# Hybrid decoder layer on one core: GpSimd's work cut into parts, the decay chain kept together, weights split one unit ahead, small inverse roots as one power on GpSimd

## The chip, the cores and the metric

The kernel runs on one core of a Trainium2 chip. A core has a matrix engine (TensorE, PE in the rows), VectorE (DVE), ScalarE (ACT), GpSimd (POOL) and SyncE (SP), which only issues transfers here. Each engine runs its own instructions strictly in order, and waits on semaphores for the others. The metric is the device time of one launch in microseconds, lower is better.

## The reference, cut to what matters

One layer for a sequence of 1024 tokens and a model width of 1024, all in float32:

```python
mod = silu(c) @ w_ada + b_ada                 # 48 columns of 128: six vectors of 1024
h = rms_norm(x) * (1 + scale1) + shift1
gq, gk, gv, gz, ga, gb, sq, sk, sv = split(h @ w_in)
gq, gk, gv = silu(causal_conv4(gq, gk, gv))   # width 4, per channel
g = -exp(a_log) * softplus(ga + dt_bias); beta = sigmoid(gb)   # per token and head
o_g = rms_norm(gated_delta_rule(l2(gq), l2(gk), gv, g, beta)) * silu(gz)   # 8 heads, chunks of 64
o_s = sliding_window(rms_norm(sq), rms_norm(sk), sv)           # 8 query, 2 key heads, window 128
x = x + gate1 * (concat(o_g, o_s) @ w_out)
h2 = rms_norm(x) * (1 + scale2) + shift2
out = x + gate2 * ((silu(h2 @ w_gate) * (h2 @ w_up)) @ w_down) # hidden width 2816
```

## The kernel before

A float32 operand is **split** into a high part (ScalarE rounds it) and a low part (the operand minus the high part, `split`, L189 to L196), and each product is three matrix passes over them (`mm3`, L213 to L215). Weights come by SP's queue as 128x1024 tiles (`wunit`); ScalarE writes their high part, GpSimd subtracts for the low part.

Tokens are in two halves of 512 columns. The order of TensorE's work is written by hand: `dense` is a chain of generators, one per projection unit, `fill(n)` runs n steps of it, and between the fills stand the visits to the other work. The order on the other engines comes from a scheduler that follows dependencies, priorities (`high_priority`) and explicit edges (`issue_after`). The stages in time are: start with norm 1 (0 to 48 us), projections with convolution and per-chunk statistics (48 to 350), recurrence and window attention (350 to 600), output projection and norm 2 (600 to 780), FFN (780 to the end).

The names that the change touches:
- `rsqrt` (L176): an inverse square root as 11 VectorE instructions on a bit trick and three Newton steps. It is called for norms (`n1_0`, `n1_1`, `n2_0`, `n2_1`, 4 columns), the window keys (`sk`, 16), window queries (`s0` to `s3`, 16), delta-rule outputs (`o0` to `o7`, 8) and the pairs of delta-rule heads (`g0` to `g3`, 32 columns).
- `mod_col` (L248 to L260): one of the columns of `mod`. On VectorE it is one instruction (L254), on GpSimd a 128x1024 product (L257) that ScalarE sums (L258); then a 128x1 bias add on VectorE (L260). `ada_some` loads and works such columns, 32 of them after the start.
- `conv` (L362 to L372): takes a projection out of PSUM. ScalarE makes the first tap, VectorE the other three (L366), and for the second half a border of 1 to 3 columns from `tails` (L372).
- `token_gen` (L630 on): the decay `g`, 24 VectorE instructions of 128x64 on `tsc`, whose result `gt` (L662) goes into the matmuls `psg` (L667).
- `pair_gen` and its helpers: `ee` (L741 on GpSimd, L743 on VectorE), `kd` (L757), `aq` (L784), and `kq` times its decay row, one 128x2048 product on GpSimd (L791). `scale_rows` (L722 to L728): ScalarE spreads an inverse root to 128x512 (`wide_k`, `wide_s`), TensorE transposes it (`psr_k`, `psr_s`), VectorE multiplies. `key_gen`: `ssk`, its inverse root `rnk`, and `kdp` on GpSimd (L864).
- `wquery_gen`: `stq` (L712, L916), its inverse root `rnq`, then `scale_rows`, then the split `ql` on GpSimd.
- `out_proj` (`w_o`, `ps_o`), and `first_half` with `modulated`, of the second norm.

Of the kernel before, what the change touches and what calls it, by code (L numbers as in the profile page):

```python
# [8 lines left out]
F32 = mybir.dt.float32  # L9
# [8 lines left out]
P = 128  # L18
# [10 lines left out]
ADA_ITER = 14  # L29
ADA_DVE = ()  # L30
# [17 lines left out]
EPS = 1e-6  # L48
NEG = -1.0e30
# [5 lines left out]
def tile_hybrid_layer(  # L55
# [134 lines left out]
    def split(hi, lo, src, eng):  # L190

        act.activation(out=r(hi), in_=src, func=AF.Copy)  # L192
        last = eng.tensor_tensor(out=r(lo), in0=src, in1=hi, op=ALU.subtract)  # L193
        if eng is pool:
            done["pool"] = last
        return last  # L196

    def wunit(src, name, kt=KT, eng=None, parts=None, raw=None, steps=1):
# [51 lines left out]
    def mod_col(u, eng=dve, bias=True):  # L250
# [5 lines left out]
        else:  # L256
            eng.tensor_tensor(out=w, in0=w, in1=cb, op=ALU.mult)  # L257
# [6 lines left out]
    def ada_some(n, tag, eng=dve):  # L264
        for u in range(ada_next[0], ada_next[0] + n):
# [5 lines left out]
            mod_col(u, eng)  # L271
# [56 lines left out]
    def modulate(hi, lo, out, x, row, a, sh, eng):  # L328
# [5 lines left out]
        else:  # L334
            done["pool"] = eng.tensor_tensor(out=out, in0=x, in1=row, op=ALU.mult)
# [177 lines left out]
    queue[dve] = rstd_done["n1_0"]  # L513
# [123 lines left out]
    def token_gen():  # L637
# [19 lines left out]
        for n in (15, 13, 11, 9, 7, 5, 3):  # L657
# [4 lines left out]
        dve.scalar_tensor_tensor(out=gt, in0=lp, scalar=-1.0, in1=bc(ealog.unsqueeze(2), (P, H, NB)),  # L662
                                 op0=ALU.mult, op1=ALU.mult)
# [69 lines left out]
    def pair_stats(p):  # L733
# [7 lines left out]
        pool.tensor_tensor(out=ee, in0=ee, in1=bc(gtok[:, 2 * p:2 * p + 2].unsqueeze(3), (P, 2, NB, HD)), op=ALU.subtract)  # L741
# [15 lines left out]
        pool.tensor_tensor(out=kd, in0=kd, in1=bc(fk.rearrange("p j b -> p b j").unsqueeze(3), (P, NB, 2, HD)), op=ALU.mult)  # L757
# [11 lines left out]
    def pair_products(p):  # L769
# [21 lines left out]
        pool.tensor_tensor(out=kb8, in0=kb8, in1=bc(eg8, (P, 16, 2, HD)), op=ALU.mult)  # L791
# [58 lines left out]
    def key_gen():  # L850
# [9 lines left out]
        for v in range(2):  # L860
            ks.append(p8.tile([P, 2, T], F32, tag="s8", name=f"ks{v}"))
            kdp = t4(f"kdp{v}", (P, NB, 2, HD), tag="c")
            for dup in range(2):
                pool.tensor_tensor(out=kdp[:, :, dup], in0=ktok[:, :, v * HD:(v + 1) * HD],  # L864
                                   in1=bc(rnk3[:, :, v:v + 1], (P, NB, HD)), op=ALU.mult)
# [45 lines left out]
    def wquery_gen(p):  # L911
# [12 lines left out]
        pool.tensor_tensor(out=r(ql), in0=q, in1=qh, op=ALU.subtract)  # L924
# [744 lines left out]
```

## Time and profile before

| what | value |
|---|---|
| time, median of 3 runs | 1305.56 us (1302.16 to 1305.72) |
| the profiled execution's own time | 1303.1 us |
| its span on the core | 1301.3 us |
| mean granted TensorE clock | 0.954 of full speed |
| busy: PE, DVE, ACT, POOL | 1193.2, 911.2, 534.7, 477.2 us |

Times in the rows are microseconds from the span's start, durations microseconds unless ns stands there. A row of the timeline is: start, duration, engine, line, operation, written tile<-read tiles, shape, how many (several of the same in a row are one row with their sum), and in brackets how long the engine stood idle before it and what ended that. A duration holds what the instruction waited inside itself.

### The profile page before, as it was taken

The page shows a single profiled execution, that of the slowest core. Times are in us where ns is not written, and L with a number is a line of the kernel's source. Part 1 is how long each engine was busy: PE and PEld are TensorE (multiplying, and loading weights), DVE is VectorE, ACT ScalarE, POOL GpSimd, SP SyncE. Part 2 cuts the span into 40 slices and gives each one's busy share as a digit, 9 for nine tenths or more (in the row PEclk, how much of TensorE's full clock was granted, in tenths as well). Part 3 has the DMA queues.
Part 4 walks back from the last instruction along what each step waited for, and adds up shares of the span by engine and source line. Part 5 has one row for each costly group of instructions (what it writes and reads, how often), then busy time and mean ns, then how long its engine had stood idle before and what let it go on. Part 6 is the DMA issues. An engine that isn't in the chain of part 4 may idle for free.

```text
span 1301.3 us, 18727 instructions
## 1 busy us (share of the span) xinstructions
PE 1193.2 (92%) x6710; PEld 979.4 (75%) x6710; DVE 911.2 (70%) x1701; ACT 534.7 (41%) x973; POOL 477.2 (37%) x343
## 2 busy tenths in 40 slices
PE   6868697796899889999999889999999999999998
PEld 5757576685788677787777668888888888788887
DVE  7999889979724667577564668877788876566420
ACT  4373555422433867534453442222222233544430
POOL 4667354534425434345554430000000015465440
PEclk8898799898899899999999899999999999999999
DMA  8726458486638955433476886555445678876651
GB/s 328 230 94 261 159 119 220 137 218 219 180 116 195 168 90 128 154 125 130 159 235 226 289 277 206 194 192 199 167 162 191 202 253 304 292 273 200 206 166 41
DMA packets 173550, 250.62 MB, mean 193 GB/s; under 512 B 41361, under 2 KB 107153, under 8 KB 171921
## 3 DMA queue, kind: packets, MB, share of 16 engines
q1 hardware_dynamic: 163856, 241.03, 57.3%
q0 software_dynamic: 9600, 8.39, 4.0%
q8 instruction: 53, 0.87, 0.3%
q14 instruction: 41, 0.33, 0.1%
HBM read 182.89 MB, written 66.45 MB: 192 GB/s over the span
## 4 chain that ended last, share of the span: by engine, by line
PE 62%; DVE 6%; ACT 4%; DMA 3%; issue 2%; POOL 1%; SPq 0%; ACTq 0%; DVEq 0%; POOLq 0%
PE ps_S L1365 8%; PE ps_S L1364 8%; PE ps_S L1363 8%; PE ps_P L1364 5%; PE ps_P L1365 5%; PE ps_P L1363 5%; PE ps_c L1363 2%; PE ps_o L213 2%; PE ps_c L1364 2%; PE ps_c L1365 2%; PE ps_o L215 2%; PE ps_o L214 2%; PE ps_gz L213 1%; DVE soltmp L818 1%; PE ps_gz L215 1%
## 5 line engine op out<-in xcount | busy, mean ns | idle before, releaser
L193 POOL TENSOR_TENSOR wP<-rP,wP 128x512 fp32r<-128x512 f32 (+1 forms) x84 | 109.3, 1313 | 394.7 <-ACT wP L192 393.1
L1364 PE MATMUL ps_P<-t,wP 128*128 128x512 f32 x308 | 120.7, 392 | 0.9 <-DVE t L193 0.9
L1363 PE MATMUL ps_P<-t,wP 128*128 128x512 f32 x308 | 120.5, 391 | 0.1
L1365 PE MATMUL ps_P<-t,wP 128*128 128x512 f32 x308 | 120.2, 390 | 0.0
L192 ACT ACTIVATE wP<-rP 128x512 fp32r<-128x512 f32 (+1 forms) x84 | 47.6, 588 | 79.3 <-PE ps_P L1365 34.4
L1363 PE MATMUL ps_c<-B,w 128*128 128x512 f32 x176 | 70.3, 399 | 8.1 <-ACT X L1407 8.1
L1364 PE MATMUL ps_c<-B,w 128*128 128x512 f32 x176 | 69.5, 395 | 0.0
L1365 PE MATMUL ps_c<-B,w 128*128 128x512 f32 x176 | 69.4, 394 | 0.0
L1364 PEld LDWEIGHTS ps_P<-t,wP 128*128 128x128 f32 x308 | 57.8, 188 | 14.0 <-DVE t L193 1.8
L1363 PEld LDWEIGHTS ps_P<-t,wP 128*128 128x128 f32 x308 | 57.8, 188 | 13.1 <-ACT t L192 0.5
L1365 PEld LDWEIGHTS ps_P<-t,wP 128*128 128x128 f32 x308 | 57.8, 188 | 12.5
L1473 ACT ACTIVATE sg<-sg 128x512 f32<-128x512 f32 x33 | 20.9, 632 | 87.8 <-DVE sg L1469 87.8
L257 POOL TENSOR_TENSOR ada<-ada,cb 128x1024 f32<-128x1024 f32 x17 | 43.8, 2592 | 29.3 <-DMA ada<-in_ada_dram 18.7
L215 PE MATMUL ps_o<-mix,w_o 128*128 128x512 f32 x128 | 50.9, 398 | 2.6 <-POOL w_o L193 2.6
L213 PE MATMUL ps_o<-mix,w_o 128*128 128x512 f32 x128 | 52.4, 409 | 0.3 <-ACT w_o L192 0.3
L1550 DVE SCALAR_TENSOR_TENSOR x1r<-ps_P,modc,x1r 128x512 f32<-128x512 f32 x16 | 11.9, 747 | 56.3 <-PE ps_P L1365 56.3
L214 PE MATMUL ps_o<-mix,w_o 128*128 128x512 f32 x128 | 50.5, 394 | 0.0
L1363 PEld LDWEIGHTS ps_c<-B,w 128*128 128x128 f32 x176 | 33.7, 191 | 17.3 <-ACT X L1407 10.3
L1365 PEld LDWEIGHTS ps_c<-B,w 128*128 128x128 f32 x176 | 33.6, 191 | 7.2
L1364 PEld LDWEIGHTS ps_c<-B,w 128*128 128x128 f32 x176 | 33.6, 191 | 6.7
L1363 PE MATMUL ps_S<-T,wS2h 128*128 128x512 f32 x88 | 35.6, 405 | 2.1 <-ACT wS2h L192 2.1
L1469 DVE TENSOR_TENSOR ops<-ps_S,xu 128x512 f32<-128x512 f32 x22 | 15.2, 690 | 30.6 <-PE ps_S L1365 20.6
(521 smaller groups left out, 3686.5 us busy)
## 6 DMA issues: line engine op xcount, KB each, us to landing
ada<-in_ada_dram SPq DMA_DIRECT2D x48, 512.0 KB, 5.0
AD<-ops SPq DMA_DIRECT2D x11, 1536.0 KB, 6.1
w<-in_wgate_dram SPq DMA_DIRECT2D x44, 256.0 KB, 3.2
w<-in_wup_dram SPq DMA_DIRECT2D x44, 256.0 KB, 3.9
rP<-SD SPq DMA_DIRECT2D x16, 704.0 KB, 5.5
sd<-in_wdown_dram SPq DMA_DIRECT2D x20, 512.0 KB, 5.3
SD<-sd SPq DMA_DIRECT2D x20, 512.0 KB, 3.8
rP<-in_wdown_dram SPq DMA_DIRECT2D x12, 704.0 KB, 6.7
```

The costliest lines, as they stand in the source:

```text
L192: act.activation(out=r(hi), in_=src, func=AF.Copy)
L193: last = eng.tensor_tensor(out=r(lo), in0=src, in1=hi, op=ALU.subtract)
L213: pe.matmul(out, lhsT=r(lhs[0]), rhs=r(rhs[0]), start=first, stop=False)
L214: pe.matmul(out, lhsT=r(lhs[0]), rhs=r(rhs[1]), start=False, stop=False)
L215: pe.matmul(out, lhsT=r(lhs[1]), rhs=r(rhs[0]), start=False, stop=last)
L257: eng.tensor_tensor(out=w, in0=w, in1=cb, op=ALU.mult)
L818: dve.tensor_tensor(out=tv[g], in0=bc(L[:, i, i + 1:32].unsqueeze(1), (P, i, 31 - i)), in1=bc(L[:, 0:i, i:i + 1], (P, i, 31 - i)), op=ALU. ...
L1363: pe.matmul(ps, lhsT=r(wh), rhs=r(xh), start=first and i == 0, stop=False, **kw)
L1364: pe.matmul(ps, lhsT=r(wh), rhs=r(xl), start=False, stop=False, **kw)
L1365: pe.matmul(ps, lhsT=r(wl), rhs=r(xh), start=False, stop=i == n - 1, **kw)
L1469: done["U"] = dve.tensor_tensor(out=out, in0=ps, in1=other, op=ALU.add)
L1473: act.activation(out=out, in_=out, func=AF.Silu)
```

## The change

1. `rsqrt` of up to 16 columns is one GpSimd instruction, x to the power of a tile that holds -0.5. That concerns 17 calls (all but `g0` to `g3`).
2. GpSimd's larger products are issued in parts of 128x512: weight splits, `mod` columns, `ql`, `kd` in 2, `kq` in 4; `ee` per head. The FFN's splits, which are 128x512 or smaller already, stay.
3. The 32 bias adds of `mod` (L260) become one 128x32 add behind the last column.
4. The decay chain is issued with high priority after 11 fills, ahead of the rest of the `mod` columns; 8 pairs of columns stand before it.
5. Each weight unit's load and split are written one unit ahead of its use (`ahead`, and `nxt` in `out_proj`).
6. In the second norm all of `modulated` is on VectorE, behind a value of the output projection; 5 instead of 6 pieces of that projection go between.

```diff
+POW_MAX = 16
+    mhalf = cp.tile([P, 16], F32, name="mhalf")
+    pool.memset(mhalf, -0.5)
     def rsqrt(out, x, n, name):
+        if n <= POW_MAX:
+            return pool.tensor_tensor(out=out, in0=x, in1=mhalf[:, 0:n], op=ALU.pow)
...
+    def pool_tt(out, in0, in1, op, n):
+        m = out.shape[1] // n
+        for i in range(n):
+            s_ = slice(i * m, (i + 1) * m)
+            done["pool"] = pool.tensor_tensor(out=out[:, s_], in0=in0[:, s_], in1=in1[:, s_], op=op)
...
-            split(parts[0][:, ks_], parts[1][:, ks_], raw[:, ks_], eng or pool)
+            split(parts[0][:, ks_], parts[1][:, ks_], raw[:, ks_], eng or pool, 2)
...
-            eng.tensor_tensor(out=w, in0=w, in1=cb, op=ALU.mult)
+            pool_tt(w, w, cb, ALU.mult, 2)
...
-            mod_col(u, eng)
+            mod_col(u, eng, False)
...
+    def ahead(units):
+        get = lambda kind, p, halves=(0, 1), *_: wunit(wmain[BASE[kind] + p], f"w_{kind}{p}_{halves[0]}")
+        w = get(*units[0])
+        for i, u in enumerate(units):
+            nxt = get(*units[i + 1]) if i + 1 < len(units) else None
+            yield from proj(*u[0:2], u[2] if len(u) > 2 else (0, 1), w, *u[3:])
+            w = nxt
...
-        pool.tensor_tensor(out=ee, in0=ee, in1=bc(gtok[:, 2 * p:2 * p + 2].unsqueeze(3), (P, 2, NB, HD)), op=ALU.subtract)
+        for j in range(2):
+            pool_tt(ee[:, j], ee[:, j], bc(gtok[:, 2 * p + j].unsqueeze(2), (P, NB, HD)), ALU.subtract, 1)
...
-        pool.tensor_tensor(out=kb8, in0=kb8, in1=bc(eg8, (P, 16, 2, HD)), op=ALU.mult)
+        pool_tt(kb8, kb8, bc(eg8, (P, 16, 2, HD)), ALU.mult, 4)
...
-    for i in range(ADA_ITER):
+    for i in range(11):
         fill(VISITS_A[0])
-        with tc.issue_after(h_done[0].ins), tc.issue_after(h_done[1].ins):
-            ada_some(1, ADA_TAGS[2 * i], pool if i not in ADA_DVE else dve)
-            ada_some(1, ADA_TAGS[2 * i + 1])
-    next(token)
+        if i < ADA_FIRST:
+            with tc.issue_after(h_done[0].ins), tc.issue_after(h_done[1].ins):
+                ada_pair()
+    with tc.high_priority():
+        next(token)
+    with tc.issue_after(done["token"].ins):
+        for i in range(11, 14):
+            fill(VISITS_A[0])
+            for _ in range(3):
+                if ada_next[0] < 44:
+                    ada_pair()
...
+    dve.tensor_tensor(out=modc[:, 16:48], in0=modc[:, 16:48], in1=b_ada[:, 16:48], op=ALU.add)
...
     def out_proj(hf):
+        nxt = wunit(wout[0], f"w_o{hf}0")
         for dt in range(KT):
-            w = wunit(wout[dt], f"w_o{hf}{dt}")
+            w = nxt
+            if dt + 1 < KT:
+                nxt = wunit(wout[dt + 1], f"w_o{hf}{dt + 1}")
...
-            modulated(f1[k], k, 0, (dve, pool)[k % 2])
+            with tc.issue_after(done["x1"].ins):
+                modulated(f1[k], k, 0, dve)
...
-        for _ in range(6):
+        for _ in range(5):
```

TensorE's rows come out in the same order as before. On VectorE the decay chain (`tsc`) stood between other work; before, its middle read as follows (L658 are seven terms of the chain's series, L366 and L372 the convolution, L254 and L260 `mod` columns):

```order
L658 SCALAR_TENSOR_TENSOR tsc<-tsc 128x64
L254 ISA ada_1135,modc<-ada_1135,cb 128x1024
L254 ISA modc 128x1
L260 TENSOR_TENSOR modc<-modc,sml 128x1
L658 SCALAR_TENSOR_TENSOR tsc<-tsc 128x64
```

and of the change the end of the chain and what follows it (lines of the changed file: L677 is L658, L681 is L662, L378 and L384 the convolution, L266 the column):

```order
L674 TENSOR_TENSOR tsc<-tsc 128x64
L675 TENSOR_SCALAR tsc<-tsc 128x64
L677 SCALAR_TENSOR_TENSOR tsc<-tsc 128x64 x7
L678 SCALAR_TENSOR_TENSOR tsc<-tsc 128x64
L680 SCALAR_TENSOR_TENSOR tsc<-tsc 128x64
L681 SCALAR_TENSOR_TENSOR tsc<-tsc 128x64
L378 SCALAR_TENSOR_TENSOR kn_628<-ps_gk_1_1090,sml,kn_628 128x511
L384 SCALAR_TENSOR_TENSOR kn_628<-tails,sml,kn_628 128x1
```

The chain's 24 instructions now stand in one piece, and two convolutions with four columns that stood inside it come behind.

The second place is GpSimd at the first window query's inverse root (`rnq` from `stq`). Before, GpSimd had there

```order
L257 TENSOR_TENSOR ada_2592<-ada_2592,cb 128x1024
L257 TENSOR_TENSOR ada_2597<-ada_2597,cb 128x1024
L193 TENSOR_TENSOR w_sq_0_2824<-w_sq_0r,w_sq_0_2824 128x1024
L980 MEMSET tx_2934 32x8x32 x2
L257 TENSOR_TENSOR ada_2602<-ada_2602,cb 128x1024
```

and of the change (L182 is the power, L200 a part of a product)

```order
L200 TENSOR_TENSOR ada_2585<-ada_2585,cb 128x512 x2
L200 TENSOR_TENSOR ada_2590<-ada_2590,cb 128x512 x2
L182 TENSOR_TENSOR rnq_2675<-stq_2656,mhalf 128x16
L200 TENSOR_TENSOR w_sq_0_2696<-w_sq_0r,w_sq_0_2696 128x512 x2
L200 TENSOR_TENSOR ada_2595<-ada_2595,cb 128x512 x2
```

The power stands behind the two columns and ahead of the weights, and the 11 VectorE instructions of this root are gone from between the solve's instructions.

## Rows read from the trace of the kernel before

**Rows 1.** Page, part 1: busy time by engine.

```profile
PE 1193.2 (92%) x6710; PEld 979.4 (75%) x6710; DVE 911.2 (70%) x1701; ACT 534.7 (41%) x973; POOL 477.2 (37%) x343
```

**Rows 2.** Stage 48 to 350 us: busy us (count) by engine, TensorE's granted clock, DMA.

```profile
48.00:350.00 302.00, 241.87 (x1374) 202.76 (x1372) 271.64 (x543) 135.06 (x228) 152.40 (x74) 0.89 0.61 182
```

**Rows 3.** TensorE's waits, 60 to 360 us: total us, times, longest us.

```profile
PE psr_s L726 <- ACT wide_s L722: 13.6, 2, 13.4
PE psg L667 <- DVE tsc L662: 11.9, 1, 11.9
PE psr_k L726 <- ACT wide_k L722: 11.4, 2, 8.8
PE ps_gk L213 <- ACT kq L388: 8.6, 1, 8.6
PE ps_kd L871 <- DVE aq L784: 4.2, 1, 4.2
PE ps_skv L213 <- DVE qt L366: 2.4, 1, 2.4
```

**Rows 4.** TensorE's waits, 600 to 780 us.

```profile
PE ps_o L215 <- POOL w_o L193: 2.6, 2, 2.1
```

**Rows 5.** Instructions by line: count, shortest/median/longest ns, first and last start.

```profile
L372 DVE SCALAR_TENSOR_TENSOR kn<-tails,sml,kn x12: 204/210/2264, 106.7 to 220.7; 128x1 f32<-128x1 f32 x4, 128x2 f32<-128x2 f32 x4, 128x3 f32<-128x3 f32 x4
...
L260 DVE TENSOR_TENSOR modc<-modc,sml x32: 91/147/2352, 98.6 to 332.7; 128x1 f32<-128x1 f32 x32
...
L257 POOL TENSOR_TENSOR ada<-ada,cb x17: 2351/2405/3252, 85.1 to 320.3; 128x1024 f32<-128x1024 f32 x17
...
L193 POOL TENSOR_TENSOR wP<-rP,wP x84: 1012/1294/3168, 1062.9 to 1273.3; 128x512 fp32r<-128x512 f32 x56, 128x384 fp32r<-128x384 f32 x28
```

**Rows 6.** GpSimd's timeline, 97 to 350 us.

```profile
118.06 9.34 POOL L257 TENSOR_TENSOR ada<-ada,cb 128x1024 f32<-128x1024 f32 x4
...
214.50 4.60 POOL L791 TENSOR_TENSOR kq<-kq,egrow 128x2048 f32<-128x2048 f32 x1
...
251.03 4.57 POOL L791 TENSOR_TENSOR kq<-kq,egrow 128x2048 f32<-128x2048 f32 x1
...
311.80 5.21 POOL L257 TENSOR_TENSOR ada<-ada,cb 128x1024 f32<-128x1024 f32 x2 [10.20 <-DMA ada<-in_ada_dram]
```

**Rows 7.** VectorE's timeline, 118 to 330 us.

```profile
118.77 1.69 DVE L372 SCALAR_TENSOR_TENSOR kn<-tails,sml,kn 128x3 f32<-128x3 f32 x1
...
131.75 0.27 DVE L642 TENSOR_TENSOR tsc<-abt,rv 128x64 f32<-128x64 f32 x1 [0.24 <-ACT abt L353]
...
138.26 2.45 DVE L652 TENSOR_SCALAR tsc<-tsc 128x64 f32<-128x64 f32 x1
...
157.41 0.21 DVE L662 SCALAR_TENSOR_TENSOR tsc<-tsc 128x64 f32<-128x64 f32 x1
...
214.57 5.61 DVE L743 TENSOR_TENSOR ee<-ee,cmask 128x1024 f32<-128x1024 f32 x1 [2.13 <-POOL ee L741]
...
251.72 3.90 DVE L372 SCALAR_TENSOR_TENSOR v<-tails,sml,v 128x1 f32<-128x1 f32 x1
...
312.16 0.67 DVE L712 TENSOR_REDUCE stq<-sq_sq 128x8 f32<-128x512 f32 x1
...
328.66 0.16 DVE L186 SCALAR_TENSOR_TENSOR rnq<-rsq_s 128x16 f32<-128x16 f32 x1
```

**Rows 8.** TensorE's timeline around the decay matmuls `psg`.

```profile
145.37 0.39 PE L215 MATMUL ps_gk<-h,w_gk 128*128 128x512 f32 x1
157.67 0.69 PE L667 MATMUL psg<-tsc,tribd 128*128 128x64 f32 x2 [11.92 <-DVE tsc L662]
...
159.54 0.63 PE L215 MATMUL ps_gk<-h,w_gk 128*128 128x512 f32 x1
```

**Rows 9.** First inverse root at the start: its first and last VectorE instruction.

```profile
14.81 0.17 DVE L180 TENSOR_SCALAR rsq_n<-ms_n 128x4 int32<-128x4 int32 x1
...
16.59 0.16 DVE L186 SCALAR_TENSOR_TENSOR rs_n<-rsq_n 128x4 f32<-128x4 f32 x1
```

More of the change, by code (lines that the diff above doesn't have):

```diff
@@ L188, in rsqrt, with split @@
         return last
-    def split(hi, lo, src, eng):
+    def pool_tt(out, in0, in1, op, n):
[3 more added lines that the diff above has]
+            done["pool"] = pool.tensor_tensor(out=out[:, s_], in0=in0[:, s_], in1=in1[:, s_], op=op)
+    def split(hi, lo, src, eng, n=1):
         act.activation(out=r(hi), in_=src, func=AF.Copy)
-        last = eng.tensor_tensor(out=r(lo), in0=src, in1=hi, op=ALU.subtract)
         if eng is pool:
-            done["pool"] = last
-        return last
+            pool_tt(r(lo), src, hi, ALU.subtract, n)
+        else:
+            return eng.tensor_tensor(out=r(lo), in0=src, in1=hi, op=ALU.subtract)
     def wunit(src, name, kt=KT, eng=None, parts=None, raw=None, steps=1):
@@ L334, in modulate @@
         else:
-            done["pool"] = eng.tensor_tensor(out=out, in0=x, in1=row, op=ALU.mult)
+            pool_tt(out, x, row, ALU.mult, 1)
             act.activation(out=r(hi), in_=out, func=AF.Identity, scale=a, bias=sh)
@@ L512, in tile_hybrid_layer @@
         rs = rstd(ps, "n1_0")
-    queue[dve] = rstd_done["n1_0"]
+    queue[pool] = rstd_done["n1_0"]
     keep_warm(WARM[1])
@@ L661, in token_gen @@
         dve.scalar_tensor_tensor(out=lp, in0=lp, scalar=2.0, in1=xa, op0=ALU.mult, op1=ALU.add)
[L662 to L663 removed]
+        done["token"] = dve.scalar_tensor_tensor(out=gt, in0=lp, scalar=-1.0, in1=bc(ealog.unsqueeze(2), (P, H, NB)),
+                                                 op0=ALU.mult, op1=ALU.mult)
         yield
@@ L863, in key_gen @@
             for dup in range(2):
-                pool.tensor_tensor(out=kdp[:, :, dup], in0=ktok[:, :, v * HD:(v + 1) * HD],
-                                   in1=bc(rnk3[:, :, v:v + 1], (P, NB, HD)), op=ALU.mult)
+                pool_tt(kdp[:, :, dup], ktok[:, :, v * HD:(v + 1) * HD], bc(rnk3[:, :, v:v + 1], (P, NB, HD)), ALU.mult, 1)
             yield
@@ L880, in tile_hybrid_layer @@
     token, keys = token_gen(), key_gen()
-    dense = chain(first, *(proj(kind, 2, (hf,), w_2[i]) for hf in range(2) for i, kind in enumerate(("gk", "gq"))), *(skv_unit(i) for i in range(4, NB)), proj("gk", 0, (1,)), proj("gq", 0, (1,)),
-                  proj("gk", 1, (1,)), proj("gq", 1, (1,)), proj("gk", 3), proj("gq", 3),
-                  *(proj("gv", p) for p in range(4)), *(proj("sq", p) for p in range(4)), proj("gz", 0, tags=("u",)), proj("gz", 1, tags=("u",)),
+    dense = chain(first, *(proj(kind, 2, (hf,), w_2[i]) for hf in range(2) for i, kind in enumerate(("gk", "gq"))), *(skv_unit(i) for i in range(4, NB)),
+                  ahead([(kind, p, (1,)) for p in range(2) for kind in ("gk", "gq")] + [("gk", 3), ("gq", 3)]
+                        + [(kind, p) for kind in ("gv", "sq") for p in range(4)]
+                        + [("gz", p, (0, 1), ("u",)) for p in range(2)]),
                   two_units((("gz", 2), ("gz", 3)), ("u",)))
@@ L923, in wquery_gen @@
         act.activation(out=r(qh), in_=q, func=AF.Copy)
-        pool.tensor_tensor(out=r(ql), in0=q, in1=qh, op=ALU.subtract)
+        pool_tt(r(ql), q, qh, ALU.subtract, 2)
         pool.dma_start(out=QS[0, p], in_=r(qh))
@@ L950, in tile_hybrid_layer @@
         if visit is v3:
-            for i in range(32 - 2 * ADA_ITER):
+            for i in range(48 - ada_next[0]):
                 ada_some(1, "b", pool if i % 4 else dve)
+    dve.tensor_tensor(out=modc[:, 16:48], in0=modc[:, 16:48], in1=b_ada[:, 16:48], op=ALU.add)
     dve.scalar_tensor_tensor(out=a2, in0=modc[:, 32:40], scalar=1.0, in1=n2w, op0=ALU.add, op1=ALU.mult)
@@ L1211, in out_proj @@
             sp.dma_start(out=x, in_=xT[dt, :, half(hf)])
-            dve.scalar_tensor_tensor(out=x, in0=ps, scalar=modc[:, 16 + dt:17 + dt], in1=x, op0=ALU.mult, op1=ALU.add)
+            done["x1"] = dve.scalar_tensor_tensor(out=x, in0=ps, scalar=modc[:, 16 + dt:17 + dt], in1=x,
+                                                  op0=ALU.mult, op1=ALU.add)
             if dt == 0:
```

13 lines of the change are left out of this document (7 added, 6 removed).

## The prediction

> **What bounds the kernel now.** I read the page's busy times first. TensorE is busy for 92% of the span, the others for at most 70% [rows 1]. So the time can fall in two ways only: where TensorE stands idle, and where its clock is granted at half. The change removes no matmul. Next I read the windows by stage. In the stage from 48 to 350 us TensorE is busy for 241.87 of 302.00 us at a mean granted clock of 0.89, while VectorE is busy for 271.64 us, that is 90% [rows 2]. Here VectorE is the bound, and GpSimd works beside it for 152.40 us. Then I read TensorE's waits in this stage: the window queries' spread inverse root (13.4 us in one piece), the decay chain (11.9), the pairs' spread inverse root (8.8 and 2.6), a projection's bank behind a convolution (8.6, and 2.4 more at the query convolution, with a second wait of that length at the key convolution), and the AQ product (4.2) [rows 3]. Every one ends on VectorE, or on a ScalarE step that VectorE released. Last I read why VectorE is late: its instructions with two operands from the on-chip memory are long only while GpSimd runs. A border step of the convolution takes 204 ns at its shortest and 2264 ns at its longest, a 128x1 bias add 91 and 2352 ns [rows 5]; the long ones are as long as a GpSimd product, 2405 ns for 128x1024 [rows 5]. The timelines show it directly. While GpSimd runs four columns from 118.06 for 9.34 us [rows 6], VectorE's border step takes 1.69 us [rows 7]; against the 4.60 us product of `kq` at 214.50 [rows 6], `ee` at 214.57 takes 5.61 us; against the one at 251.03 [rows 6], a 128x1 step takes 3.90 us [rows 7]. So VectorE waits for the end of GpSimd's instruction, and about one VectorE instruction gets in per boundary between two of GpSimd's.
>
> By the Trainium skill, "SBUF — State Buffer", section "Who interferes with whom", a VectorE instruction with two SBUF inputs contends with a GpSimd instruction that reads SBUF, as a lock for the whole instruction. The trace agrees: 3.90 us instead of about 0.2.
>
> **The change part by part.** The sum is made against the profiled execution, 1303.1 us, which lies 2.5 below the median of the runs.
>
> *Parts of 512.* A 128x512 part takes about 1.29 us (the median of the FFN's splits, which are that size) where a 128x1024 product takes 2.41 [rows 5], so two parts cost 0.18 us more on GpSimd, which has room (152.40 of 302 us [rows 2]). What VectorE waits at most falls from 2.4 to 1.3 us, and at `kq` from 4.6 to 1.3. Bounds: nothing, if each VectorE instruction merely waits twice as often, and the whole wait at the other end. By place: the product of `kq` in four saves `ee` about 4.6 - 1.3 = 3.3 us, and with the 16-column root of `sk` gone from among VectorE's rows some 0.7 more (four or five steps of 0.16 [rows 9]), so 4 of the 8.8 us at `psr_k`. The other `psr_k` wait, 2.6 us, falls by 1.5. At 251.72 a 128x1 step falls from 3.90 to at most about 1.3 + 0.2, so 2.8 of the 4.2 us at `ps_kd` go. The two waits of 2.4 us at the convolutions fall by 3.5 together, since every border step there waits for one product (1.69 us) and would wait for a part, and the bias adds between are gone. The wait of 8.6 us falls by 1.5; it hangs on VectorE's second half of `h` too, which stays.
>
> *The decay chain.* It begins at 131.75 and ends at 157.41 + 0.21, 25.9 us for 24 instructions of some 0.21 us, or 5 us of work; three are held for 2.3 to 2.5 us, as at 138.26 (2.45), and the rest of the time goes to convolutions and columns that stand between [rows 7]. TensorE comes to `psg` at 157.67 - 11.92 = 145.75 [rows 8]. In one piece the chain needs about 5 us, some 3 for the ScalarE steps in it (an estimate), and waits behind GpSimd's parts: with 4 to 6 of these, 5 to 8 us. So it ends 13 to 16 us after 131.75, at 145 to 148. The wait falls from 11.9 to about 2: a gain of 10. Bounds: if all 24 waited for a part of 1.29 us it would end at 131.75 + 5 + 31 = 168, 10 us later than now; but that needs 24 parts of GpSimd's work ready in that time, and the columns are held back behind the chain. With no wait it gains the whole 11.9. What is late next: the two convolutions of `kn` and `qt` that stood inside the chain now come behind it, and their PSUM banks come free some 3 us later. Among TensorE's waits only those of 8.6 and 2.4 us are for such a bank [rows 3]; I put 2 us on it.
>
> *The inverse roots on GpSimd.* 17 calls take 187 VectorE instructions away and add 17 on GpSimd. At the start the 11 instructions run from 14.81 to 16.59 + 0.16, that is 1.94 us [rows 9]. No row shows a power on GpSimd. Bounds: 0.16 us, as one such VectorE instruction [rows 9], and 2.41, a whole 128x1024 product [rows 5]. I take 1 us, between, since it has at most 16 columns but is another operation. Where it matters is `s0`: the sums are ready at 312.16 + 0.67, the root only at 328.66 [rows 7], 15.8 us later, since the 11 steps alternate with the solve's and wait for GpSimd. As one instruction it stands on GpSimd behind two columns that run from 311.80 for 5.21 us [rows 6], in four parts then. So it starts at about 317.5 and ends at 318.5, where it now ends at 328.66 + 0.16: 10.3 us earlier, of the 13.4 us that TensorE waits behind it [rows 3]. Since what stands ahead on GpSimd also waits for a transfer of its own (10.20 us [rows 6]), I count 7. Calls `s1` to `s3` and `o0` to `o7` lie under other matmuls, and their VectorE work is hidden as before; nothing for them. At the start I put 0, with 1 either way.
>
> *Weights a unit ahead.* TensorE waits for weights for 2.6 us at `ps_o` [rows 4] and nowhere else that matters: 2. *The bias adds*: their price is in the waits above. *The second norm's edit*: four 128x512 products go from GpSimd to VectorE, which is idle for 30% of the span [rows 1]; nothing, and up to 4 x 0.67 = 2.7 us against it (by the 128x512 reduction at 312.16 [rows 7]) if TensorE waits there.
>
> *The sum.* Idle time: 1.5 + 3.5 + 10 + 1.5 + 4 + 2.8 + 7 + 2 = 32.3. Behind a wait the clock is at half for some microseconds: a matmul at 159.54 takes 0.63 us, at 145.37 0.39 [rows 8], 0.24 us apart. With three waits gone for good, at some five or six matmuls each, 4 is an estimate for it. Against that stand 2 for the convolutions behind the chain and 8 for what I can't place: power and parts in GpSimd's queue ahead of `ee`, `kd` and `kdp`, and the stage's work moving closer to VectorE's own limit (271.64 us of work and waits in a stage that would last 275 [rows 2], of which the waits must shrink for it to fit). 1303.1 - 32.3 - 4 + 10 = 1276.8. I say 1277.
>
> **The rivals.**
> *The waits are only dealt out anew* (0.17). VectorE then waits twice as often for half as long; only what leaves VectorE counts: the roots of `s0` (7), part of the chain's regrouping (5), weights (2). 1303 - 14 + 4 for the parts' cost = 1293. For it: one VectorE instruction gets in at each boundary [rows 6, 7]. Against: at `kq` a single instruction waits for 4.6 us, and a second wait doesn't follow.
> *The power is dear* (0.08). Slower: it ends on the other side if one power holds GpSimd, and with it VectorE, for long. Some eight calls stand on TensorE's path (norms, `sk`, `s0`, and the outputs that come last). To eat the 26 us, each must cost 2 + 26/8 = 5.3 us; at 7 us, three times the dearest row above, the time is 1277 + 8 x 5 = 1317 less what is hidden, about 1312. Nothing in the rows is that dear on GpSimd save `kq`'s 4.60.
> By the Trainium skill, "GPSIMD Engine Reference", section "2.1 Instruction dispatch", the first call of a freshly loaded GpSimd routine pays about 6 us for its code; no run here shows it. By that the start alone would be some 5 us longer, 1282.
> *Banks behind the chain* (0.10). The convolutions that come behind it, and the columns behind those, make TensorE wait for PSUM where it did not: the 10 us come back. 1287. For it: such waits of 8.6 and 2.4 us exist [rows 3].
> *The change does not do what it says* (0.07). The products in parts still hold VectorE and the power waits behind transfers in GpSimd's queue, as the 10.20 us do [rows 6]: 1301 to 1304.
>
> **How the numbers follow.** The forecast has 0.58, the rivals 0.17, 0.08, 0.10 and 0.07. A measurement of this kernel tells about 0.3% from no change, that is 3.9 us around 1305.6. The forecast and the cases at 1287 and 1293 are faster: 0.85, less 0.01 for their upper ends. Same: 0.09, most of the case without effect and some of the dear power. Slower: 0.07. The forecast's own range is 1264 to 1288: 8 more if all waits named go, 11 less if the upper bounds of power and parts hold. The range for all is 1260 to 1302, which leaves out the slow case and the best.
>
> **What would show it.** In the changed profile the wait at `psg` is at most 4 us; the longest wait of `psr_s` is at most 6; `ee` takes at most 3 us on VectorE; no 128x1 step takes over 1.5; the power rows on GpSimd are about 1 us; the granted clock from 48 to 350 us rises to about 0.93. It is wrong if a power takes over 3 us, if VectorE's border steps still take 2 us, or if a new wait on PSUM banks stands behind the chain.

## The result and the profile after

The changed kernel takes 1287.07 us (median of 4 runs, 1285.41 to 1288.89) against 1303.86 for the kernel before (4 runs): a ratio of 0.9876, with a 95% interval of 0.9853 to 0.9900. It is faster by 16.8 us in the medians, 13 to 19 us by the interval. The forecast was 1277 with a range of 1264 to 1288, so the direction is right, the time lies 1 us inside the upper end of the range, and 10 us of the expected gain are missing.

Page, part 1 of the changed kernel, which answers to [rows 1]:

```profile
PE 1192.2 (93%) x6710; PEld 980.0 (76%) x6710; DVE 855.9 (66%) x1487; ACT 534.5 (42%) x973; POOL 525.9 (41%) x434
```

VectorE has 55 us less, GpSimd 49 us more. The window of the stage from 48 to 350 us, which answers to [rows 2]:

```profile
48.00:350.00 302.00, 253.96 (x1486) 211.20 (x1485) 251.21 (x474) 141.30 (x238) 188.28 (x140) 0.92 0.65 191
```

TensorE does 12 us more in the same stretch, and its mean granted clock rises from 0.89 to 0.92. TensorE's waits of the changed kernel between 60 and 345 us (in us: total, times, longest), which answer to [rows 3]:

```profile
PE pst L697 <- ACT gst L691: 10.4, 1, 10.4
PE psr_k L745 <- ACT wide_k L741: 8.5, 2, 7.0
PE psr_s L745 <- ACT wide_s L741: 7.6, 2, 6.1
PE ps_gk L225 <- ACT kq L400: 7.6, 1, 7.6
PE ps_gk L227 <- POOL w_gk L200: 3.6, 1, 3.6
PE pst_sq L728 <- DVE qs L747: 2.8, 2, 2.0
PE ps_gk L225 <- ACT w_gk L204: 1.6, 1, 1.6
...
PE pst L697 <- ACT gst L690: 1.2, 1, 1.2
...
PE psg L686 <- DVE tsc L681: 0.8, 1, 0.8
PE ps_kd L890 <- DVE aq L804: 0.3, 1, 0.3
```

The decay chain's wait at `psg` fell from 11.9 to 0.8 us, `ps_kd` from 4.2 to 0.3, `psr_s` from 13.4 to 6.1, and the two convolution waits are gone. But at the top stands a wait that did not exist: 10.4 us at `pst`, the transposes of `gst`, which VectorE and ScalarE make from the result of `psg`. Also new are 3.6 + 1.6 us for the weights `w_gk`.

TensorE's rows are in the same order in both kernels, so the start of the same matmul can be compared. The table is from both timelines of TensorE:

| matmul | before, us | after, us | earlier by |
|---|---|---|---|
| `ps_skv` behind the query convolution | 125.97 | 117.50 | 8.5 |
| `ps_gk`, third pass, waits for `w_gk` | 141.97 | 137.49 | 4.5 |
| `psg` | 157.67 | 145.11 | 12.6 |
| second `pst` | 162.84 | 160.63 | 2.2 |
| `psr_k`, the long wait | 229.30 | 224.84 | 4.5 |
| `ps_kd` behind `aq` | 257.03 | 244.97 | 12.1 |
| first `psr_s` | 329.54 | 307.58 | 22.0 |
| second `psr_s` | 345.45 | 329.65 | 15.8 |
| `ps_S` behind `wS2h` | 778.25 | 764.43 | 13.8 |
| end of the span | 1301.3 | 1287.2 | 14.1 |

The gain comes in four steps (the convolutions before 126 us, the decay chain up to `psg`, the pairs from 185 to 260, the root `s0`), and three times a part of it is handed back: 4.0 us at `w_gk`, 10.4 of 12.6 us between `psg` and `pst`, and 6.2 us behind `s0`. Behind 345 us nothing more is gained: 15.8 us there, 14.1 at the end.

Why `pst` is late stands in VectorE's timeline of the changed kernel (L681 ends the chain, L378 and L384 are convolutions, L266 are columns, L688 is the copy from `psg` into `gst`):

```profile
144.83 0.23 DVE L681 SCALAR_TENSOR_TENSOR tsc<-tsc 128x64 f32<-128x64 f32 x1
144.98 0.74 DVE L378 SCALAR_TENSOR_TENSOR kn<-ps_gk,sml,kn 128x511 f32<-128x511 f32 x1
145.64 0.21 DVE L384 SCALAR_TENSOR_TENSOR kn<-tails,sml,kn 128x1 f32<-128x1 f32 x1
145.76 1.22 DVE L266 CUSTOM_DVE_ANT_0 ada<-ada,cb 128x1024 f32<-128x1024 f32 x1
...
154.64 1.22 DVE L266 CUSTOM_DVE_ANT_0 ada<-ada,cb 128x1024 f32<-128x1024 f32 x1
155.78 0.08 DVE L266 DVE_READ_ACCUMULATOR2_ANT modc<- 128x1 f32 x1
155.78 0.74 DVE L378 SCALAR_TENSOR_TENSOR qt<-ps_gq,sml,qt 128x509 f32<-128x509 f32 x1
156.44 0.21 DVE L384 SCALAR_TENSOR_TENSOR qt<-tails,sml,qt 128x3 f32<-128x3 f32 x1
156.57 0.21 DVE L688 COPY gst<-psg 128x64 f32<-128x64 f32 x1
```

`psg` runs at 145.11, but the copy of its result stands behind two convolutions and six columns and starts at 156.57: what was taken out of the chain now stands between the chain's result and its first use. Why TensorE waits for `w_gk` stands in GpSimd's timeline, where 14 column parts are ahead of its split. The split itself begins 2.1 us earlier than before (136.16 against 138.25), but TensorE comes to it 8.4 us earlier. Two later rows of the same view are read further below:

```profile
115.75 20.46 POOL L200 TENSOR_TENSOR ada<-ada,cb 128x512 f32<-128x512 f32 x14
136.16 2.50 POOL L200 TENSOR_TENSOR w_gk<-w_gk_1r,w_gk 128x512 fp32r<-128x512 f32 x2
...
303.79 3.07 POOL L182 TENSOR_TENSOR rnq<-stq,mhalf 128x16 f32<-128x16 f32 x1
306.83 7.36 POOL L200 TENSOR_TENSOR w_sq<-w_sq_0r,w_sq 128x512 fp32r<-128x512 f32 x2
```

The power, and VectorE's border step and `ee`, by line (count, shortest/median/longest ns, first and last start), the latter two answering to [rows 5, 7]:

```profile
L182 POOL TENSOR_TENSOR fo<-so,mhalf x8: 1635/1644/1683, 383.8 to 563.1; 128x8 f32<-128x8 f32 x8
L182 POOL TENSOR_TENSOR rs_n<-ms_n,mhalf x4: 1006/1014/1033, 16.0 to 633.0; 128x4 f32<-128x4 f32 x4
L182 POOL TENSOR_TENSOR rnq<-stq,mhalf x4: 2926/3002/3175, 303.8 to 357.8; 128x16 f32<-128x16 f32 x4
...
L384 DVE SCALAR_TENSOR_TENSOR kn<-tails,sml,kn x12: 205/620/1303, 106.1 to 215.9; 128x1 f32<-128x1 f32 x4, 128x2 f32<-128x2 f32 x4, 128x3 f32<-128x3 f32 x4
...
L763 DVE TENSOR_TENSOR ee<-ee,cmask x4: 1209/2172/2306, 178.5 to 229.5; 128x1024 f32<-128x1024 f32 x4
```

A power costs 1.0, 1.6 and 3.0 us for 4, 8 and 16 columns (the 17th call, the keys' `rnk`, 2.90). The border step's longest wait fell from 2.26 to 1.30 us, the length of a part, and its median rose from 0.21 to 0.62: it waits more often for less. `ee` takes at most 2.31 us where it took 5.61.

### The profile page after: what moved, and what is told of

The parts are those of the page before. It is cut to its first block, busy times and chain, and to the rows that moved or that the text cites. A ratio compares the mean times of both kernels' runs of the same rounds, so it can differ in the third digit from the quotient of the medians.

```text
span 1287.2 us, 18639 instructions
## 1 busy us (share of the span) xinstructions
PE 1192.2 (93%) x6710; PEld 980.0 (76%) x6710; DVE 855.9 (66%) x1487; ACT 534.5 (42%) x973; POOL 525.9 (41%) x434
## 4 chain that ended last, share of the span: by engine, by line
PE 61%; DVE 19%; DMA 10%; ACT 5%; issue 2%; SPq 2%; POOL 1%; DVEq 0%; ACTq 0%; POOLq 0%
PE ps_S L1404 7%; PE ps_S L1402 7%; PE ps_S L1403 7%; PE ps_P L1403 5%; PE ps_P L1402 5%; PE ps_P L1404 5%; PE ps_o L225 2%; PE ps_o L227 2%; PE ps_o L226 2%; PE ps_c L1402 2%; PE ps_c L1403 2%; PE ps_c L1404 2%; DVE ada L458 1%; DMA rP<-in_wdown_dram 1%; DMA sd<-in_wdown_dram 1%
## 5 line engine op out<-in xcount | busy, mean ns | idle before, releaser
L200 POOL TENSOR_TENSOR wP<-rP,wP 128x512 fp32r<-128x512 f32 (+1 forms) x84 | 110.1, 1324 | 394.7 <-ACT wP L204 393.3
L200 POOL TENSOR_TENSOR ada<-ada,cb 128x512 f32<-128x512 f32 x34 | 50.5, 1517 | 19.1 <-DMA w_gz_0r<-in_wmain_dram 10.7
L1589 DVE SCALAR_TENSOR_TENSOR x1r<-ps_P,modc,x1r 128x512 f32<-128x512 f32 x16 | 11.9, 747 | 54.6 <-PE ps_P L1404 54.6
L1404 PE MATMUL ps_S<-T,wS2l 128*128 128x512 f32 x88 | 35.6, 404 | 1.0 <-DVE wS2l L208 1.0
```

Source lines behind the costliest of these rows:

```text
L200: done["pool"] = pool.tensor_tensor(out=out[:, s_], in0=in0[:, s_], in1=in1[:, s_], op=op)
L1404: pe.matmul(ps, lhsT=r(wl), rhs=r(xh), start=False, stop=i == n - 1, **kw)
L1589: dve.scalar_tensor_tensor(out=x, in0=src, scalar=g2(dt), in1=x, op0=ALU.mult, op1=ALU.add)
```

## The experiments

My theory: the parts carry the gain, and the missing 10 us are the pieces handed back at `pst` and at `w_gk`, each because an instruction that TensorE needs stands behind columns in its engine's queue. The rival: the stage is bound by what VectorE and GpSimd have to do together, so any regrouping only moves the waits. Every time below stands with its ratio to the kernel before, measured on the same chip, and the 95% interval of the ratio; the changed kernel's ratio is 0.9876 (0.9853 to 0.9900). Starts of matmuls are read from one profiled execution of each kernel. Executions of one kernel lie up to 11 us apart (e15: 1287.49 to 1298.53), so the end of one trace counts for less than the ratio.

**e1: the late columns behind `gst`.**

```diff
-        dve.tensor_tensor(out=ed.rearrange("p h b -> p (h b)"), in0=psg[:, 64:128], in1=gst[:, 2], op=ALU.subtract)
+        done["gst"] = dve.tensor_tensor(out=ed.rearrange("p h b -> p (h b)"), in0=psg[:, 64:128], in1=gst[:, 2],
+                                        op=ALU.subtract)
...
             fill(VISITS_A[0])
-            for _ in range(3):
-                if ada_next[0] < 44:
-                    ada_pair()
...
             next(visit)
+        if n_visit == 0:
+            with tc.issue_after(done["gst"].ins):
+                while ada_next[0] < 44:
+                    ada_pair()
```

> The changed kernel, with the last six pairs of mod columns issued behind VectorE's ed (the instruction behind the copy of psg into gst) instead of behind the decay chain; everything else as changed. Theory: the 10 us that the chain gave at psg came back at pst (10.4 us), because the copy into gst stands on VectorE behind six columns of 1.22 us and two convolutions. Then the copy comes some 7 us earlier, the wait at pst falls to 3 to 5 us, and the time to 1280 to 1283. Rival: the stage is bound by what VectorE and GpSimd have to do together, so the columns delay the next wait by as much as they leave here; then 1285 to 1289.

Measured: 1284.74 us, ratio 0.9833 (0.9794 to 0.9873), against 0.9876. The waits at `pst` are gone from the list (0.03 us); `pst` starts at 153.12, 5.9 us earlier than in the changed kernel, though TensorE waits 3.2 + 0.8 us for `w_gq` on its way there, which it did not before. The next wait then grows, in TensorE's waits from 60 to 345 us:

```profile
PE psr_k L746 <- ACT wide_k L742: 11.5, 2, 6.8
```

The first `psr_k` starts at 181.21, only 1.1 us earlier than in the changed kernel. So the copy's place was the cause of the wait at `pst`, and most of what its move gave only moved on, as the rival says: the second `pst` starts 7.2 us earlier than in the changed kernel, the first `psr_s` 2.7 us earlier (304.89). At the end of the profiled execution it is 5.6 us (span 1281.6); where the difference comes from behind `s0` is not shown. The time lies between the two expectations, and its interval overlaps that of the change.

**e6: as e1, and GpSimd's columns behind the splits of `w_gk` and `w_gq`.**

```diff
             fill(VISITS_A[0])
+    w_last = done["pool"]
...
-            with tc.issue_after(done["gst"].ins):
+            with tc.issue_after(done["gst"].ins), tc.issue_after(w_last.ins):
```

> As e1, and the GpSimd columns of these pairs stand on GpSimd behind the splits of w_gk and w_gq. Theory: the new wait of 3.6 + 1.6 us for w_gk comes from the 14 column parts (20.5 us) that GpSimd does ahead of that split, and with it gone TensorE comes earlier to psg, the chain waits for fewer parts too; 1275 to 1279, no wait for w_gk. Rival (bound by VectorE and GpSimd together): 1284 to 1288.

Measured: 1281.03 us, ratio 0.9801 (0.9763 to 0.9838). This interval lies clear of that of the change: it is the fastest kernel of the study, 24 us below before. `psg` starts at 135.75, 9.4 us earlier than in the changed kernel, and the second `pst` at 143.19, 17.4 earlier. None of it is left at the first `psr_s` (308.70, 1.1 us later than in the changed kernel), since two new waits come; so the time lies between what the two theories gave. The span is 8.6 us shorter even so, because the lead comes back behind `s0`: 1.8 us at the second `psr_s`, 7.2 at the `ps_S` of the table above. So the six runs show that e6 is faster, and the trace shows that the waits at `pst` and at the first `w_gk` go (2.4 us are left at `pst`); that the time saved is the time of these waits is not shown. TensorE's waits from 60 to 345 us:

```profile
PE psr_s L746 <- ACT wide_s L742: 19.4, 2, 15.6
PE psr_k L746 <- ACT wide_k L742: 9.8, 3, 6.1
PE ps_gk L227 <- POOL w_gk L200: 8.0, 1, 8.0
```

GpSimd's timeline has both causes: the columns now stand ahead of the next `w_gk`, and four parts ahead of the power of `s0` take 13.30 us instead of about 5, one of them alone 9.20 us. The last two rows are VectorE's, the end of the solve's run of dense instructions:

```profile
140.61 15.88 POOL L200 TENSOR_TENSOR ada<-ada,cb 128x512 f32<-128x512 f32 x8
156.45 2.51 POOL L200 TENSOR_TENSOR w_gk<-w_gk_0r,w_gk 128x512 fp32r<-128x512 f32 x2
...
291.82 13.30 POOL L200 TENSOR_TENSOR ada<-ada,cb 128x512 f32<-128x512 f32 x4 [11.53 <-DMA w_gz_0r<-in_wmain_dram]
305.07 2.91 POOL L182 TENSOR_TENSOR rnq<-stq,mhalf 128x16 f32<-128x16 f32 x1
...
300.60 0.66 DVE L842 TENSOR_TENSOR lanes<-lanes,soltmp 128x220 f32<-128x220 f32 x2
301.17 0.37 DVE L839 TENSOR_TENSOR soltmp<-lanes 128x210 f32<-128x210 f32 x1
```

**e8: as e6, and the power of `s0` ahead of the last four columns.**

```diff
-        rsqrt(rn.rearrange("p a b -> p (a b)"), st.rearrange("p a b -> p (a b)"), 16, f"s{p}")
+        done["rnq"] = rsqrt(rn.rearrange("p a b -> p (a b)"), st.rearrange("p a b -> p (a b)"), 16, f"s{p}")
...
-        if visit is v3:
-            for i in range(48 - ada_next[0]):
-                ada_some(1, "b", pool if i % 4 else dve)
+        if visit is q0 and ada_next[0] < 48:
+            with tc.issue_after(done["rnq"].ins):
+                for i in range(48 - ada_next[0]):
+                    ada_some(1, "b", pool if i % 4 else dve)
```

> As e6, and the last four mod columns are issued behind the first window query's inverse root, so that the power stands on GpSimd ahead of the column parts. In e6 these four parts took 13.3 us at 291.8 to 305.1, while VectorE ran the solve, and the power began at 305.07 although its sums were ready at about 293.6; TensorE waited 15.6 us for wide_s. Theory: the queue position decides; the power begins at 293 to 295, the longest wait of psr_s falls to 3 to 7 us, and the time to 1272 to 1276. Rival: the solve keeps GpSimd out whatever stands first in its queue, then the power itself takes 8 us or more and the time stays at 1279 to 1283.

Measured: 1285.76 us, ratio 0.9864 (0.9830 to 0.9898); the longest wait of `psr_s` is 10.9 us. The rival's mechanism holds: the power begins at 295.11 as planned and takes 10.62 us itself. GpSimd's row, and below it VectorE's rows of the same microseconds (L839 and L842 are the solve, a product and a sum of two operands from the on-chip memory each):

```profile
295.11 10.62 POOL L182 TENSOR_TENSOR rnq<-stq,mhalf 128x16 f32<-128x16 f32 x1 [12.15 <-DVE stq L952]
```

```profile
295.26 0.72 DVE L839 TENSOR_TENSOR soltmp<-lanes 128x240 f32<-128x240 f32 x2
295.89 0.72 DVE L842 TENSOR_TENSOR lanes<-lanes,soltmp 128x240 f32<-128x240 f32 x2
296.53 0.72 DVE L839 TENSOR_TENSOR soltmp<-lanes 128x240 f32<-128x240 f32 x2
```

VectorE's instructions follow each other every 0.32 us and are not slowed, while GpSimd does not get in. The solve's run ends at 302.96 and the power at 305.73. Where a power stands helps little as long as this run lasts. The shorter wait gains nothing that lasts: TensorE is 2.3 us ahead of e6 at the first `psr_s` and 3.0 us behind it at 345 us. The profiled execution is e8's fastest of six (1281.10 us), and the two intervals just overlap, so whether e8 is slower than e6 is not shown.

**e2 and e4: which powers pay.** In e2 all roots are back on VectorE (`POW_MAX = 0`, and the start's queue entry for VectorE again), in e4 those of 16 columns (the edit shown is that of e4).

```diff
-POW_MAX = 16
+POW_MAX = 8
```

> The changed kernel with all inverse roots on VectorE again (11 instructions each), the rest as changed. Theory: the power takes 3.0 us for 16 columns, more than 11 instructions alone, but at s0 it replaces steps that alternated with the solve's, so the longest wait of psr_s goes back from 6.1 to 11 to 14 us; 1291 to 1296. Rival: the gain at s0 came from the parts, and a power that holds GpSimd and VectorE for 3 us takes back what it gives; 1284 to 1289.

> The changed kernel, with the power for up to 8 columns only; the five roots of 16 columns (sk, s0 to s3) on VectorE again. Theory: what the power is worth (4.3 us between the changed kernel and all roots on VectorE) comes from s0; 1289 to 1293. Rival: a power of 16 columns takes 3.0 us and pays nothing, the gain is in the 4- and 8-column ones; 1284 to 1288.

Measured: e2 1291.41 us, ratio 0.9900 (0.9868 to 0.9932); e4 1290.57 us, 0.9902 (0.9871 to 0.9933). Both lie where the theories put them. The two are alike, so nothing is seen of the powers of 4 and 8 columns, and what the power is worth (0.24 to 0.26% of 1304, some 3 us by the medians) would lie in the 16-column calls. Both intervals overlap that of the change, so the times alone don't show this gain. TensorE's waits of e2 show where it would come from:

```profile
PE psr_s L745 <- ACT wide_s L741: 16.6, 2, 14.6
```

That is 14.6 us against 6.1, and the same `psr_s` starts 11.0 us later than in the changed kernel; of these 11 some 4 are left by 420 us, and 2.5 in the span.

**e3 and e7: the parts.** In e3 the changed kernel's products are whole again (`n = 1` in `pool_tt`); e7 is the kernel before with the parts alone (`pool_tt` and its six calls from the diff above).

```diff
     def pool_tt(out, in0, in1, op, n):
+        n = 1
         m = out.shape[1] // n
```

> The changed kernel with GpSimd's products whole again (128x1024, kq 128x2048, ee per head still), the rest as changed. Theory: VectorE's border steps and ee wait 2.4 and 4.6 us again, the two convolution waits of 2.4 us and those at psr_k and ps_kd come back; 1293 to 1298. Rival: the waits are only dealt out anew, and parts cost 0.18 us each; 1284 to 1289.

> The kernel before, with GpSimd's products in parts as in the change and nothing else. Theory: the parts carry most of the change, as the 13 us that the whole products cost in the changed kernel; 1289 to 1295, with the waits of 2.4 us at the convolutions gone and ee at most 2.4 us. Rival: the parts pay only with the columns held back behind the chain; 1298 to 1303.

Measured: e3 1300.31 us, ratio 0.9956 (0.9931 to 0.9981), so without the parts 0.8% of the change's 1.24% are gone. e7 1297.67 us, ratio 0.9969 (0.9947 to 0.9991): alone they give only 0.31%. Both are some 2.5 us above what I expected, and e7 is next to its rival's 1298. In e3 the border step and `ee` are as long as before the change, by line:

```profile
L385 DVE SCALAR_TENSOR_TENSOR kn<-tails,sml,kn x12: 202/210/1990, 107.3 to 219.7; 128x1 f32<-128x1 f32 x4, 128x2 f32<-128x2 f32 x4, 128x3 f32<-128x3 f32 x4
...
L764 DVE TENSOR_TENSOR ee<-ee,cmask x4: 1206/2502/5602, 180.9 to 234.9; 128x1024 f32<-128x1024 f32 x4
```

In e7 they are short (1.26 and 2.28 us at most), but the decay chain is still cut up and ends no earlier: `psg` starts at 158.80, 1.1 us later than before, though TensorE comes to it 2.5 us earlier. TensorE's waits of e7:

```profile
PE psr_s L733 <- ACT wide_s L729: 17.2, 2, 14.0
PE psg L674 <- DVE tsc L669: 15.6, 1, 15.6
```

**e5 and e11: the power alone, the chain alone, in the kernel before.** e5 is before with the power branch in `rsqrt` (and the start's queue entry for GpSimd); e11 is before with the loop of 11 fills, `ADA_FIRST = 8`, the chain at high priority and the rest of the columns behind it.

```diff
+        if n <= 16:
+            return pool.tensor_tensor(out=out, in0=x, in1=mhalf[:, 0:n], op=ALU.pow)
```

> The kernel before, with the inverse roots of up to 16 columns as a power on GpSimd and nothing else. Theory: the wait of 13.4 us at s0 falls by 4 to 7 us, the rest is hidden; 1297 to 1301. Rival: GpSimd's whole products stand ahead of the power and the power holds VectorE for 3 us; 1303 to 1307.

> The kernel before, with the decay chain issued as in the change (8 pairs of columns ahead, high priority, the rest behind it) and nothing else. Theory: the wait at psg falls from 11.9 to at most 5 us, and the gain comes back at pst, behind the copy into gst, so the time falls by less than 4 us: 1299 to 1304. Rival: the chain's regrouping is worth its 10 us by itself, and what took them back in the changed kernel were the parts; 1291 to 1296.

Measured: e5 1300.78 us, ratio 0.9976 (0.9951 to 1.0001), so 3 us or nothing: TensorE's wait at `psr_s` falls from 13.4 to 2.9 us, and 7.0 us come at `pst_sq` behind it. e11 1308.23 us, ratio 1.0028 (1.0006 to 1.0049): alone, the regrouping of the chain makes the kernel slower, which neither expectation had. TensorE's waits of e11 from 60 to 345 us:

```profile
PE pst L677 <- ACT gst L671: 8.6, 1, 8.6
...
PE pst L677 <- ACT gst L670: 5.7, 1, 5.7
...
PE psg L666 <- DVE tsc L661: 2.7, 1, 2.7
```

9.2 us are won at `psg`, and 14.3 us lost at `pst`. The second `pst` starts at 166.53, 3.7 us later than before, and 3.8 us later is also where the profiled execution ends (span 1305.1).

**e12: weights not ahead.**

```diff
-        w = get(*units[0])
-        for i, u in enumerate(units):
-            nxt = get(*units[i + 1]) if i + 1 < len(units) else None
-            yield from proj(*u[0:2], u[2] if len(u) > 2 else (0, 1), w, *u[3:])
-            w = nxt
+        for u in units:
+            yield from proj(*u[0:2], u[2] if len(u) > 2 else (0, 1), get(*u), *u[3:])
...
     def out_proj(hf):
-        nxt = wunit(wout[0], f"w_o{hf}0")
         for dt in range(KT):
-            w = nxt
-            if dt + 1 < KT:
-                nxt = wunit(wout[dt + 1], f"w_o{hf}{dt + 1}")
+            w = wunit(wout[dt], f"w_o{hf}{dt}")
```

> The changed kernel, with each weight unit loaded and split at its use as before, not one unit ahead. Theory: the two waits at ps_o (2.6 us before) come back and little else; 1289 to 1292. Rival: the splits written ahead also crowd GpSimd's queue in front of ee, kd and the powers, so without them nothing is lost or something gained; 1283 to 1288.

Measured: 1288.99 us, ratio 0.9883 (0.9853 to 0.9912), which can't be told from the change. The waits at `ps_o` don't come back, and the one for `w_gk` is 3.6 us here too: no effect of writing the units ahead is seen in either direction.

**e15 and e14: the columns spread.** e15 is e6 with one pair of the late columns behind each of the next visits; e14 is e15 with `s0` to `s3` on VectorE, their visits at high priority and the last four columns later.

```diff
-        if n_visit == 0:
-            with tc.issue_after(done["gst"].ins), tc.issue_after(w_last.ins):
-                while ada_next[0] < 44:
-                    ada_pair()
+        if ada_next[0] < 44:
+            with tc.issue_after(done["gst"].ins), tc.issue_after(done["pool"].ins):
+                ada_pair()
```

> As e6, with the last six pairs of columns spread, one pair behind each of the next visits, instead of all behind gst. In e6 TensorE waits 8.0 us for w_gk, which stands on GpSimd behind four columns (15.9 us). Theory: that wait falls below 2 us, and the time to 1274 to 1279. Rival: the columns then stand ahead of ee, kd and kq, whose waits (psr_k, ps_kd) grow by as much; 1280 to 1285.

> As e15, with the four roots s0 to s3 on VectorE again, their visits at high priority, and the last four columns written behind the third window query. In e8 the power of s0 alone took 10.6 us beside the solve's dense run of two-operand instructions, where it takes 3.0 otherwise. Theory: the solve keeps GpSimd out, and the 11 steps between the solve's own instructions need only 6 to 9 us, so the longest wait of psr_s is 5 to 9 us, and the time 2 to 6 us below e15. Rival: the steps wait for GpSimd's column parts as before the change, the wait is 12 to 15 us and the time that of e15 or above.

Measured: e15 1292.78 us, ratio 0.9903 (0.9872 to 0.9935); e14 1291.74 us, 0.9906 (0.9879 to 0.9932). In e15 the wait for `w_gk` is gone as expected, and worth 6 us there; then the rival's mechanism holds, and the time is some 8 us above even the rival's range. Its GpSimd timeline in the pairs' stretch:

```profile
198.24 3.53 POOL L200 TENSOR_TENSOR ada<-ada,cb 128x512 f32<-128x512 f32 x2 [4.75 <-DMA ada<-in_ada_dram]
...
207.81 11.10 POOL L200 TENSOR_TENSOR kq<-kq,egrow 128x512 f32<-128x512 f32 x8 [1.55 <-DMA egrow<-R]
```

Columns that wait for their own transfer stand ahead of `ee` and `kq`, the waits at `psr_k` grow to 16.3 us, and TensorE, 6.1 us ahead of e6 at `w_gk`, is 13.4 us behind it at `ps_kd` (249.65 against 236.28). In e14 the longest wait of `psr_s` is 13.8 us: VectorE's steps beside the solve are no faster than the power held up by it, and my expectation of 5 to 9 us fell.

## Why the prediction was right, and what it missed

**What bounds the kernel**: right. The time fell from 48 to 350 us, where VectorE's waits for GpSimd were cut: of the 14.1 us at the end, all were there by 345 us (15.8).

**Parts of 512**: right in mechanism. The longest wait of a border step is 1.30 us, of `ee` 2.31; `ps_kd` lost 3.9 us (2.8 expected). At `psr_k` the wait fell by 1.9 where I had 4, but it ends 4.5 us earlier: TensorE itself came 2.6 us earlier. The rival that waits are dealt out anew is partly true, since the border step's median trebled.

**The decay chain, "what is late next"**: this is the step that failed. The gain at `psg` was 11.1 us (10 expected). For what comes late behind it I named the banks of two convolutions and put 2 us; the runs show 11.6 us at `pst`, because the first use of `psg` on VectorE stands behind what was taken out of the chain, the two convolutions and six columns. Moving the columns takes that wait away (0.03 us left in e1, 2.4 in e6), and e11 shows it without any other edit. The rival "banks behind the chain" had the right amount (10 us back, 1287) with the wrong instruction: no bank was waited for. I had looked at who waits for the chain, and not at the next instruction of the same generator.

**Weights a unit ahead**: the 2.6 us at `ps_o` went, but they are gone without this edit too (e12), and the parts alone leave 1.1 of them (e7); which edit takes them is open. Instead 5.2 us came at `w_gk`, behind columns in GpSimd's queue, which I had only in a lump of 8 us.

**The sum**: it was made against the profiled execution, and there 1288.9 stands against 1276.8, 12.1 us more. The lump and the 2 make 10; the new waits at `pst`, `w_gk` and `pst_sq` alone are 11.6 + 5.2 + 2.8 = 19.6, which is 9.6 more. The 4 us for the clock hardly came: TensorE's busy time for the same 6710 matmuls fell only from 1193.2 to 1192.2 us, since behind the new waits too a matmul takes 0.63 us instead of 0.39 for a while (as at 161.33). That is 3 us more, and what the waits that went gave beyond the 32.3 takes 1 to 2 back. The time fell inside the range by 1 us with a term missed by 9.6, which is luck as much as margin. The lower end of that range does not follow from its own words either: 8 less than 1277 is 1269, not 1264.

**The inverse roots**: the wait at `psr_s` fell by 7.3 us, as the 7 that I took, and that is partly luck. The price was mis-sized: 3.0 us for 16 columns, not 1. At `s0` it lies on TensorE's path: the power began at 303.79 and ended at 306.86, and `psr_s` started at 307.58. And of what the power gives there (8.5 us of the wait by e2) only some 3 are left at the end. By the Trainium skill, "GPSIMD Engine Reference", section "2.1 Instruction dispatch", the first call of a freshly loaded routine pays some 6 us for loading code. The trace shows no such time at this operation's first call, which starts 0.2 us behind the end of the VectorE instruction that it waits for (15.72 + 0.15) and takes 1.03 us:

```profile
16.03 1.03 POOL L182 TENSOR_TENSOR rs_n<-ms_n,mhalf 128x4 f32<-128x4 f32 x1 [11.86 <-DVE ms_n L290]
```

Nor does the power hold VectorE at `s0` (last section), and 3.0 us is far from the 5.3 that the rival needed, so the rival that it is dear fell.

**The signs named in advance**: `psg` (0.8 us), `ee` (2.31), the 128x1 steps of this stage (1.30) and the clock (0.92 for about 0.93) came as said. The longest wait of `psr_s` is 6.1 where I had at most 6, and the power is 3.0 us where I had 1. One call of 3.18 us even meets the sign "a power takes over 3 us", though the loss that it should tell of did not come. The new wait behind the chain is there, but not on a bank.

**What each edit is worth alone**: parts 0.31%, power 0.24% (its interval reaches no change at all), chain -0.28%; all six edits together 1.24%. The three make 0.27%, so most of the gain comes from edits that act together or from those not tried alone. One such pair shows in the traces: with parts alone the cut-up chain lets TensorE start `psg` only at 158.80, the chain alone hands 14.3 us back at `pst`, and both together leave 0.8 + 11.6 there. What the merged bias adds and the second norm's edit give by themselves was not tried; the 32 bias adds, of up to 2.35 us each [rows 5], stay a rival for a part of the gain.

## What to carry to other kernels

When a chain is pulled together, follow its result to the next instruction on the same engine: what was moved out of the chain may stand right there, and the stall only changes its name. On an engine that runs in order, look for a place for work without a deadline (here the columns of `mod`) behind the short steps that another engine waits for, copies and weights included, and then look at what it stands ahead of now: in e6 that was the next weights (8.0 us), in e15 `ee` and `kq`. And price an edit by where the end of a wait moves, not by how the wait's length changes, since the one who waits arrives earlier too.

## What the runs showed of the hardware

GpSimd and VectorE keep each other out unequally. While GpSimd's products follow each other, about one VectorE instruction with two operands from the on-chip memory gets in per boundary [rows 6, 7]. While VectorE's two-operand instructions of the solve follow each other every 0.32 us, a GpSimd instruction issued among them waits for the end of the run. A power of 3.0 us took 10.62 (e8), one part of 1.3 us took 9.20 (e6), and in the changed kernel, of the two parts of `w_sq` that took 7.36 us at 306.83, one alone took 6.04. These three ended 2.8, 1.1 and 1.1 us behind the end of the solve's run, about what they take undisturbed. By the Trainium skill, "SBUF — State Buffer", section "Who interferes with whom", the port pair that the two engines share is an exclusive lock, and the order of issue decides who blocks. The waits of single instructions here agree with that (3.90 us at 251.72 [rows 7]); that a whole run of VectorE keeps GpSimd out was seen in these three cases.

Once begun, a power of 16 columns let VectorE run, which is not what a lock for the whole instruction would do. While the power ran from 303.79 to 306.86 in the changed kernel, the solve's instructions took 0.31 to 0.33 us each from 304.01 on, as they do alone; why is open:

```profile
304.01 0.74 DVE L838 TENSOR_TENSOR soltmp<-lanes 128x240 f32<-128x240 f32 x2
304.67 0.71 DVE L841 TENSOR_TENSOR lanes<-lanes,soltmp 128x240 f32<-128x240 f32 x2
```
